# Scores from fp16 pairs in place of fp32r pairs, and an earlier opening of the projection's buffers

## The chip, the cores and the metric

The kernel runs on one core of a Trainium2 chip. The metric is the device time of one execution in microseconds (us); lower is better. The kernel before was timed three times: 886.39, 886.42 and 890.78 us, median 886.42 us. TensorE is PE in the profile, its weight loads are PEld, VectorE is DVE, ScalarE is ACT, GpSimd is POOL, and SyncE (which only issues transfers here) is SP.

## The reference

One layer of an encoder with 2064 tokens (16 meta tokens and 2048 real ones), width 1024, in float32:

```
u = rmsnorm(h, norm_g) @ w_in                # 1024 -> 1984 columns, split in six
pool_in, pool_gate, c_q, c_kv, k_r, attn_gate = split(u)
pool_out = silu(pool_gate) * pool_mixer(pool_in)      # trailing means 2/4/8/16 minus the token
q = rmsnorm(c_q) @ w_q_b                     # 4 heads x (128 plain + 64 rotary)
k, v = split(rmsnorm(c_kv) @ w_kv_b)         # 4 heads x (128 + 128); one shared rotary key from k_r
s = (q_nope.k_nope + q_rope.k_rope) * 192**-0.5
p = softmax(where(key chunk <= query chunk, s, min))  # chunks of 64 tokens, meta tokens ahead
attn_out = silu(attn_gate) * (p @ v)
h = h + concat(pool_out, attn_out) @ w_out
return rmsnorm(h, final_norm_g)[16:]
```

## The kernel before, in words

Precision is kept by splitting a float32 value into a high and a low part and summing three products (high by high, high by low, low by high). Where the parts are `F32R` (a float32 read by TensorE in one pass) they take 4 bytes an element; where they are `F16` they take 2.

The work runs in three stages.

1. **Tokens** (`phase0`, `post0`): in 17 tiles of 128 tokens the latent columns (query 256, key/value 128, rotary 64) are projected from `xh`, `xl` and `wth`, `wtl`. `post0` takes the two norms from a Square on ScalarE and a power on GpSimd, applies the rotation to the shared key, and transposes the result on TensorE. The keys end as a pair in `klo` (keys 0 to 1039) and `khi` (the rest), each with a latent part and a rotary part. `prep_attention` loads the attention weights, and `absorb` multiplies the query and key weights into one matrix per head (`weh`, `wel`), so that a query meets the 128 latent key columns directly. `qprep(g)` makes the queries of 256 tokens as pairs `qh`, `ql` (latent) and `qr` (rotary, high and low in the two halves of the partitions).
2. **Attention rows** (`step(c, p)`: chunk `c` of 64 queries, `p` is a pair of heads, so 128 query rows). `scores` cuts the visible keys into pages of up to 4 tiles and blocks of up to 512 keys. For a block five matmuls add into one PSUM bank (lines 440 to 444), VectorE takes the maximum (446), ScalarE the exponential (467) and its fp16 high part (470), GpSimd or VectorE the low part (472), and SyncE issues a transfer that transposes the page (479). `pv` of the chunk before follows one chunk later and multiplies the transposed pages by the values (503). Six PSUM banks (tag `s`) hold score blocks and projection results in turn. Pages sit in rings of buffers `p`, `hl` and `pt`, drawn from the pools `att1`, `att2` and `att3`; `set_pages` says which pools are in the ring. Chunks 0 to 7 run beside the token stage; then come 23 to 20, 27 to 24, 31 to 28, 19 to 16 (the long rows, in the order of `ORDER`), and 15 down to 8. After chunk 28 `att2` leaves the ring; after chunk 19 (`CLOSE`) it is closed, and the pool `c1` of the projection opens in its place.
3. **Projection** (`pair`, `op_prep`, `op`): the remaining columns of `w_in` in fp16 pairs and the output projection. Its first pieces are put among the rows by two tables: `PREP` says after which chunk weights are loaded (`a`), scaled and split (`b`) and token columns loaded (`x`); `FILL` says after which chunk one `pair` of column groups (48 matmuls of 256) is computed. The order of the rest is the string `TAIL`.

The framework's planner puts the instructions of each engine in a fixed order; each engine then runs its own list in that order, and SyncE's transfers too are issued in order.

Of the kernel before, what the change touches and what calls it, by code (L numbers as in the profile page):

```python
# [8 lines left out]
F32 = mybir.dt.float32  # L9
# [32 lines left out]
ATT2 = (3, 2, 3)  # L42
# [3 lines left out]
FILL = {15: 1, 13: 1, 11: 1}  # L46
# [17 lines left out]
LASTLONG = 28  # L64
CLOSE = 19
# [4 lines left out]
PREP = {18: 'a4', 17: 'b4 x0', 16: 'a5', 15: 'b5', 14: 'x1', 12: 'x2', 10: 'a0'}  # L70
# [21 lines left out]
def hymba(tc, hT, hcat, tab, w_tok, w_m, w_out, wqT, wqr, wkT, wv, pool_w,  # L92
# [38 lines left out]
    nc.gpsimd.memset(inv2[:, 1:2], 1.0 / 128.0)  # L131
# [19 lines left out]
    klo = kv.tile([P, 2, 2, KLO + META], F32R, name="klo")  # L151
    kx_cm, kx = open_pool("kx", side="right")
    khi = kx.tile([P, 2, 2, L - KLO], F32R, name="khi", tag="khi", bufs=1, padded_shape=[P, 2, 2, 1088])
# [11 lines left out]
    gks = kv.tile([P, 1], F32, name="gks")  # L165

# [51 lines left out]
    load_rest(1)  # L218

# [31 lines left out]
    def post0(j):  # L251
# [11 lines left out]
        nc.gpsimd.tensor_scalar(out=st[:T], in0=st[:T], scalar1=EPS, scalar2=None, op0=ALU.add)  # L263
# [12 lines left out]
        nc.scalar.mul(out=vh[:T, j], in_=u[:T, 256:384], mul=SV)  # L276
        nc.vector.scalar_tensor_tensor(out=vl[:T, j], in0=u[:T, 256:384], scalar=SV, in1=vh[:T, j], op0=ALU.mult, op1=ALU.subtract)
# [17 lines left out]
    def prep_attention():  # L295
# [12 lines left out]
    def absorb(wk_r, gk_bc, wq_r, wr_r, wv_r):  # L308
        nc.vector.tensor_scalar(out=gqa, in0=gq_t, scalar1=ALPHA, scalar2=None, op0=ALU.mult)
        nc.vector.tensor_scalar(out=gks, in0=gkv_t, scalar1=UNSCALE, scalar2=None, op0=ALU.mult)  # L310
        nc.vector.tensor_tensor(out=wk_r, in0=wk_r, in1=gk_bc.rearrange("p (o c) -> p o c", o=1).broadcast_to([P, H, P]), op=ALU.mult)
        for i in range(2):
# [5 lines left out]
            nc.vector.scalar_tensor_tensor(out=wel[:, i], in0=pw, scalar=gqa[:, i:i + 1], in1=f(weh[:, i]), op0=ALU.mult, op1=ALU.subtract)  # L318
            nc.scalar.mul(out=wrh[:, i], in_=wr_r[:, i], mul=gqa[:, i:i + 1])
            nc.vector.scalar_tensor_tensor(out=wrl[:, i], in0=wr_r[:, i], scalar=gqa[:, i:i + 1], in1=f(wrh[:, i]), op0=ALU.mult, op1=ALU.subtract)  # L320
# [5 lines left out]
    def qprep(g):  # L326
# [5 lines left out]
        qh = qp.tile([P, 4, H, CH], F32R, name=f"qh{g}", tag="qh", bufs=2)  # L332
        ql = qp.tile([P, 4, H, CH], F32R, name=f"ql{g}", tag="ql", bufs=2)
        qr = qp.tile([P, 4, H, CH], F32R, name=f"qr{g}", tag="qr", bufs=2)
        for hp in range(2):
# [10 lines left out]
            nc.vector.tensor_sub(out=ql[:, :, 2 * hp:2 * hp + 2].rearrange("p c h t -> p h c t"), in0=ps, in1=f(dst))  # L346
# [22 lines left out]
        for s in range(2):  # L369
            for e in range(2):  # L370
# [3 lines left out]
                nc.vector.tensor_sub(out=dst[64:128], in0=src, in1=f(dst[0:64]))  # L374
# [33 lines left out]
    def scores(c, p):  # L408
# [43 lines left out]
        nc.vector.tensor_scalar(out=nb_, in0=nm, scalar1=LNP, scalar2=None, op0=ALU.add)  # L452
        for pg, (base, m, blocks) in enumerate(pages):
# [12 lines left out]
            for o, w, _, _, bi in blocks:  # L466
                nc.scalar.activation(out=pr[:, o:o + w], in_=pss[bi][:, :w], func=AF.Exp, bias=nb_,  # L467
# [89 lines left out]
    def load_x(i):  # L557
        o, n = SUBS[i]
        if i == 0:
            x = cw["pool"].tile([P, 2 * KT * n], F16, name="x0", tag="x0", bufs=1)  # L560
        else:
            if i == 1:
                cw["x"] = kx.tile([P, 2, 4352], F16, name="xx", tag="khi", bufs=1)
            x = cw["x"][:, i % 2, :2 * KT * n]
# [262 lines left out]
    att2_cm, att2 = open_pool("att2", side="right")  # L827
# [22 lines left out]
    flush()  # L850
    close_pool(att3_cm)
# [85 lines left out]
```

## Time and profile before

| | profiled execution |
|---|---|
| its time | 889.79 us |
| its span, first to last instruction | 888.0 us |
| mean granted TensorE clock | 0.978 |
| PE busy | 848.8 us (96%) |
| PEld busy | 684.0 us |
| DVE busy | 536.8 us |
| ACT busy | 480.6 us |
| POOL busy | 321.3 us |

The busy time of PE counts each matmul from its start to its modelled end, and matmuls overlap, so a row's mean is longer than the distance from one matmul's start to the next; rates are read from the distances. A wait row says which engine stood idle at which line, until which instruction, for how long in all, how often, and the longest. The granted clock is 1.00 at 2.4 GHz and 0.50 at 1.2 GHz.

### The profile page before, as it was taken

How to read it: one execution, taken by the hardware profiler on the slowest of the kernel's cores; microseconds unless marked ns; L12 is line 12 of the kernel's file. 1: busy time of each engine (PE TensorE's matmuls, PEld its weight loads, DVE VectorE, ACT ScalarE, POOL GpSimd, SP SyncE). 2: the span in 40 equal slices, each digit the busy share in tenths (PEclk: the TensorE clock that was granted, in tenths of full speed). 3: DMA queues.
4: the chain of work that ended last, by engine and by line, in shares of the span. 5: the costliest groups of instructions: out<-in, count | busy, mean ns of one | idle time of the engine just before them, and what ended most of it. 6: DMA issues, size and time to landing. Idle time of an engine off the chain costs nothing. (4 is left out here: it accounts for less than half of the span.)

```text
span 888.0 us, 16286 instructions
## 1 busy us (share of the span) xinstructions
PE 848.8 (96%) x5835; PEld 684.0 (77%) x5835; DVE 536.8 (60%) x1268; ACT 480.6 (54%) x1268; POOL 321.3 (36%) x512
## 2 busy tenths in 40 slices
PE   9979989999999999898888998999999999999996
PEld 8969968889888888787877897866666666667644
DVE  6657769856757667878624578775455344435242
ACT  6656756757777667785634684854242332232321
POOL 2666642434545453645313124641141121111100
PEclk9989999999999999998999999999999999999998
DMA  8755525977798788884786112212133122111111
GB/s 287 219 170 161 163 46 100 175 145 136 131 148 150 137 153 155 168 156 130 147 180 247 48 55 76 75 26 76 48 90 107 48 72 72 48 49 48 48 40 56
DMA packets 206956, 101.80 MB, mean 115 GB/s; under 512 B 169257, under 2 KB 196363, under 8 KB 206875
## 3 DMA queue, kind: packets, MB, share of 16 engines
q1 hardware_dynamic: 187392, 93.30, 44.0%
q10 hardware_dynamic: 19483, 7.47, 3.7%
q8 instruction: 46, 0.75, 0.4%
q14 instruction: 35, 0.29, 0.1%
HBM read 55.60 MB, written 8.43 MB: 72 GB/s over the span
## 5 line engine op out<-in xcount | busy, mean ns | idle before, releaser
L633 PEld LDWEIGHTS <-w 128*128 128x128 f16 x2304 | 226.8, 99 | 36.7 <-ACT w L617 2.3
L633 PE MATMUL mp<-xx,w 128*128 128x256 f16 x2016 | 229.4, 275 | 0.6 <-DVE gt L662 0.6
L765 PE MATMUL op<-wo,mh 128*128 128x512 f16 (+1 forms) x792 | 168.1, 373 | 0.0
L765 PEld LDWEIGHTS <-mh 128*128 128x128 f16 x792 | 77.5, 98 | 85.5
L472 POOL TENSOR_TENSOR hl<-p,hl 128x512 f16<-128x512 f32 (+4 forms) x104 | 105.0, 1031 | 94.9 <-ACT hl L470 94.8
L467 ACT ACTIVATE p<-s,st 128x512 f32<-128x512 f32 (+8 forms) x168 | 99.4, 600 | 63.2 <-DVE st L452 53.0
L446 DVE TENSOR_REDUCE st<-s 128x1 f32<-128x512 f32 (+6 forms) x154 | 88.7, 589 | 19.0 <-PE s L444 17.5
L503 PE MATMUL o<-pt,vh 128*128 128x256 f16 x544 | 92.2, 274 | 2.3 <-DMA pt<-hl 2.3
L470 ACT CAST hl<-p 128x512 f16<-128x512 f32 (+6 forms) x168 | 82.5, 541 | 4.1 <-DMA pt<-hl 3.9
L769 ACT ACTIVATE osq<-xr 128x512 f16<-128x512 f32 (+1 forms) x33 | 20.4, 617 | 100.0 <-DVE xr L767 78.0
L503 PE MATMUL o<-pt,vl 128*128 128x256 f16 x272 | 74.4, 274 | 0.0
L660 ACT ACTIVATE th<-mp,whalf 128x256 f32<-128x256 f32 x64 | 30.0, 469 | 72.6 <-PE mp L633 58.7
L767 DVE SCALAR_TENSOR_TENSOR xr<-op,mmx,xr 128x512 f32<-128x512 f32 (+1 forms) x33 | 24.2, 734 | 72.4 <-PE op L765 72.4
L503 PEld LDWEIGHTS <-vh 128*128 128x128 f16 x544 | 52.1, 98 | 11.6 <-issue 2.6
L771 POOL TENSOR_SCALAR oss<-oss 128x1 f32<-128x1 f32 x16 | 3.9, 246 | 154.6 <-DVE oss L770 154.6
L472 DVE TENSOR_TENSOR hl<-p,hl 128x512 f16<-128x512 f32 (+7 forms) x64 | 50.6, 792 | 8.1 <-ACT hl L470 7.5
L440 PE MATMUL s<-klo,qh 128*128 128x512 f32 (+9 forms) x116 | 46.2, 398 | 8.5 <-ACT p L467 5.4
L573 DVE SCALAR_TENSOR_TENSOR yr<-yr,gxs,rbc 128x256 f32<-128x256 f32 (+1 forms) x64 | 35.5, 617 | 15.8 <-DMA yr<-hT_in 15.7
L441 PE MATMUL s<-klo,qh 128*128 128x512 f32 (+9 forms) x116 | 43.5, 375 | 0.0
L442 PE MATMUL s<-klo,ql 128*128 128x512 f32 (+9 forms) x116 | 43.5, 375 | 0.0
L444 PE MATMUL s<-klo,qr 128*128 128x512 f32 (+9 forms) x116 | 43.2, 373 | 0.0
L577 POOL TENSOR_TENSOR xx<-yr,xx 128x512 f16<-128x512 f32 x28 | 36.0, 1299 | 19.8 <-ACT xx L576 19.8
(229 smaller groups left out, 1756.6 us busy)
## 6 DMA issues: line engine op xcount, KB each, us to landing
xt<-hcat_in SPq DMA_DIRECT2D x16, 512.0 KB, 6.7
xr<-hcat_in SPq DMA_DIRECT2D x16, 512.0 KB, 3.8
raw<-hT_in SPq DMA_DIRECT2D x15, 512.0 KB, 5.0
out_dram<-xr SPq DMA_DIRECT2D x15, 512.0 KB, 2.7
yr<-hT_in SPq DMA_DIRECT2D x14, 512.0 KB, 3.8
wr<-w_m_in SPq DMA_DIRECT2D x12, 512.0 KB, 4.2
rb<-rd ACTq DMA_DIRECT2D x32, 128.0 KB, 4.6
wor<-w_out_in SPq DMA_DIRECT2D x8, 512.0 KB, 6.5
```

The lines of the kernel that those rows point to most:

```text
L440: nc.tensor.matmul(ps[:, :w], lhsT=q(qh), rhs=kt[:, 0, 0, sl], start=True, stop=False)
L441: nc.tensor.matmul(ps[:, :w], lhsT=q(qh), rhs=kt[:, 1, 0, sl], start=False, stop=False)
L442: nc.tensor.matmul(ps[:, :w], lhsT=q(ql), rhs=kt[:, 0, 0, sl], start=False, stop=False)
L444: nc.tensor.matmul(ps[:, :w], lhsT=q(qr), rhs=kt[:, 1, 1, sl], start=False, stop=True)
L446: nc.vector.reduce_max(out=mx[:, bi:bi + 1], in_=ps[:, :w], axis=AX.X)
L467: nc.scalar.activation(out=pr[:, o:o + w], in_=pss[bi][:, :w], func=AF.Exp, bias=nb_, accum_out=sm[:, bi:bi + 1] if nb > 1 else tot)
L470: nc.scalar.copy(out=hl[:, 0, sl], in_=pr[:, sl])
L472: eng.tensor_tensor(out=hl[:, 1, sl], in0=pr[:, sl], in1=hl[:, 0, sl], op=ALU.subtract)
L503: nc.tensor.matmul(ps[:, :2 * P], lhsT=v, rhs=x, start=i == 0, stop=i == len(ops) - 1)
L577: nc.gpsimd.tensor_tensor(out=xl[:, k:k + 2], in0=xr[:, k - k0:k - k0 + 2], in1=xh[:, k:k + 2], op=ALU.subtract)
L633: nc.tensor.matmul(ps[:, :n - sk], lhsT=a[:, k], rhs=x[:, k, sk:n], start=e == 0, stop=e == 3 * KT - 1)
L765: nc.tensor.matmul(ps[:, :w], lhsT=x[:, k], rhs=y[:, sl], start=i == 0, stop=i == 3 * KT - 1)
```

## The change

Keys (`klo`, `khi`) and queries (`qh`, `ql`, `qr`) become fp16 pairs. The value scale moves into the norm of the key/value latent (`inv2`, `eps2`), the rotary key is scaled by a power of two `kd` taken from the norm of its weight columns, and `absorb` scales the combined query weights by a power of two `tt` taken from the sums of their squares. The exponential then multiplies its input by the inverse, `tinv`, a column of 128 values, and the maximum is scaled likewise. The buffers of the queries are half as large, and the staging of the first tokens and of two weights uses other buffers. `att2` stays open to the end of the rows with two `pt` buffers in place of three, `c1` opens before the long rows, and `PREP` and `FILL` name earlier chunks. The second and third blocks of token columns (`x1`, `x2`) get separate buffers, where one buffer in `khi`'s place held both.

```diff
-ATT2 = (3, 2, 3)
+ATT2 = (3, 2, 2)
-FILL = {15: 1, 13: 1, 11: 1}
+FILL = {19: 1, 15: 1, 11: 1}
-LASTLONG = 28
-CLOSE = 19
-PREP = {18: 'a4', 17: 'b4 x0', 16: 'a5', 15: 'b5', 14: 'x1', 12: 'x2', 10: 'a0'}
+PREP = {20: 'a4', 27: 'b4', 24: 'x0', 31: 'a5', 28: 'b5', 17: 'x1', 13: 'x2', 10: 'a0'}
...
-    klo = kv.tile([P, 2, 2, KLO + META], F32R, name="klo")
+    klo = kv.tile([P, 2, 2, KLO + META], F16, name="klo")
-    khi = kx.tile([P, 2, 2, L - KLO], F32R, ...)
+    khi = kx.tile([P, 2, 2, L - KLO], F16, ...)
...
+    fj = ap.tile([P, KT, 64], F16, name="fj", tag="fj", bufs=1)
+    nc.scalar.activation(out=fj, in_=f(wth[:, :, 384:448]), func=AF.Square, accum_out=fk[:, 0:1])
+    pf = bank("m", "pf")
+    nc.tensor.matmul(pf[:, 0:1], lhsT=ones, rhs=fk[:, 0:1], start=True, stop=True)
+    ...  (maximum on DVE, power on POOL, three more on DVE: kd and its inverse)
...
-        nc.gpsimd.tensor_scalar(out=st[:T], in0=st[:T], scalar1=EPS, scalar2=None, op0=ALU.add)
+        nc.gpsimd.tensor_tensor(out=st[:T], in0=st[:T], in1=eps2[:T], op=ALU.add)
+        nc.gpsimd.tensor_scalar(out=rk, in0=r, scalar1=kd[:T], scalar2=None, op0=ALU.mult)
...
-        wr_r = ap.tile([P, 2, 256], F32, name="wr_r", tag="raw", bufs=2, padded_shape=[P, 2, 512])
+        wr_r = qp.tile([P, 2, 256], F32, name="wr_r", tag="qr", bufs=2)
-        wv_r = ap.tile([P, H, P], F32, name="wv_r", tag="raw", bufs=2, padded_shape=[P, KT, P])
+        wv_r = qp.tile([P, H, P], F32, name="wv_r", tag="ql", bufs=2)
...
     # absorb, per half i, after the four matmuls into pw:
-            nc.scalar.mul(out=weh[:, i], in_=pw, mul=gqa[:, i:i + 1])
+            for e, src in ((4, pw), (6, wr_r[:, i])):
+                nc.scalar.activation(out=junk, in_=src, func=AF.Square, scale=gqa[:, i:i + 1], accum_out=fk[:, e + i:e + i + 1])
     # absorb, once:
+        nc.tensor.matmul(pf[:, 0:4], lhsT=ones, rhs=fk[:, 4:8], start=True, stop=True)
+        ...  (two on DVE, power on POOL, six on DVE: tt, tinv, gqe, gqr)
+        for i, pw in enumerate(pws):
+            nc.scalar.mul(out=weh[:, i], in_=pw, mul=gqe[:, i:i + 1])
...
-        qh = qp.tile([P, 4, H, CH], F32R, name=f"qh{g}", tag="qh", bufs=2)
+        qh = qp.tile([P, 4, H, CH], F16, name=f"qh{g}", tag="qh", bufs=2)      # ql, qr likewise
...
-        nc.vector.tensor_scalar(out=nb_, in0=nm, scalar1=LNP, scalar2=None, op0=ALU.add)
+        nc.vector.tensor_scalar(out=nb_, in0=nm, scalar1=tinv, scalar2=LNP, op0=ALU.mult, op1=ALU.add)
-                nc.scalar.activation(out=pr[:, o:o + w], in_=pss[bi][:, :w], func=AF.Exp, bias=nb_,
+                nc.scalar.activation(out=pr[:, o:o + w], in_=pss[bi][:, :w], func=AF.Exp, scale=tinv, bias=nb_,
...
-    att2_cm, att2 = open_pool("att2", side="right")
+    att2_cm, att2 = open_pool("att2", side="left")
+    c1_cm, c1 = open_pool("c1", side="right")
+    pre_c(c1)
...
-        if c == LASTLONG:
-            set_pages((att1, ATT1), (att3, ATT3))
-        if c == CLOSE:
-            close_pool(att2_cm)
-            c1_cm, c1 = open_pool("c1", side="right")
-            pre_c(c1)
```

## Rows read from the trace of the kernel before

**Rows 1.** Busy time, clock and DMA share in three stretches (us).

```profile
core 0: us, PE busy (x) PEld busy (x) DVE busy (x) ACT busy (x) POOL busy (x), PEclk, DMA share, GB/s
38.00:56.00 18.00, 12.39 (x66) 10.84 (x66) 11.13 (x29) 13.20 (x37) 10.72 (x23) 0.85 0.59 174
150.00:344.00 194.00, 191.26 (x1272) 168.69 (x1271) 134.79 (x318) 138.27 (x396) 90.39 (x115) 1.00 0.83 150
344.00:464.00 120.00, 107.07 (x789) 94.97 (x788) 82.88 (x202) 75.49 (x213) 53.21 (x68) 0.94 0.73 146
```

**Rows 2.** Timeline of PE, score matmuls in long rows: start, length (us), instruction.

```profile
294.81 0.34 PE L440 MATMUL s<-khi,qh 128*128 128x384 f32 x1
...
295.69 0.38 PE L440 MATMUL s<-khi,qh 128*128 128x464 f32 x1
...
296.76 0.39 PE L440 MATMUL s<-klo,qh 128*128 128x512 f32 x1
...
297.91 0.39 PE L440 MATMUL s<-klo,qh 128*128 128x512 f32 x1
...
308.58 0.28 PE L440 MATMUL s<-khi,qh 128*128 128x272 f32 x1
...
309.20 0.39 PE L440 MATMUL s<-klo,qh 128*128 128x512 f32 x1
```

**Rows 3.** Timeline of PE, fp16 matmuls of the projection, unbroken runs merged.

```profile
585.76 1.91 PE L633 MATMUL mp<-xx,w 128*128 128x256 f16 x16
587.51 4.70 PE L765 MATMUL op<-wo,mh 128*128 128x512 f16 x21
```

**Rows 4.** Line 440 (first of five matmuls of a block): ns min/median/max, widths.

```profile
L440 PE MATMUL s<-klo,qh x116: 281/393/689, 61.7 to 444.1; 128*128 128x512 f32 x68, 128*128 128x384 f32 x12, 128*128 128x272 f32 x8, 128*128 128x336 f32 x6
...
L440 PE MATMUL s<-khi,qh x52: 199/338/497, 145.7 to 353.9; 128*128 128x384 f32 x12, 128*128 128x272 f32 x8, 128*128 128x464 f32 x6, 128*128 128x400 f32 x6
```

**Rows 5.** ACT by line and form: busy us, mean ns, idle before.

```profile
L467 ACT ACTIVATE p<-s,st 128x512 f32<-128x512 f32 x72 | 48.9, 685 | 51.3 <-DVE st L452 44.0 <-DMA rb<-rd 4.2 <-POOL hl L472 1.7
...
L467 ACT ACTIVATION_READ_ACCUMULATOR p<-s,st 128x1 f32 x168 | 33.9, 202 | 0.0
...
L664 ACT ACTIVATE gt<-mp,winv 128x256 f32<-128x256 f32 x32 | 14.9, 466 | 0.0
...
L505 ACT CAST oh<-o 128x256 fp32r<-128x256 f32 x32 | 12.0, 375 | 11.1 <-PE o L503 10.9
```

**Rows 6.** ACT by line, 344 to 464 us.

```profile
L467 ACT ACTIVATE p<-s,st 128x384 f32<-128x384 f32 (+7 forms) x40 | 23.0, 578 | 10.7 <-DVE st L452 6.4 <-DVE hl L472 2.6 <-issue 1.5
...
L590 ACT ACTIVATE wa<-wr 128x512 f16<-128x512 f32 x6 | 3.8, 642 | 4.8 <-DMA wr<-w_m_in 4.8
L617 ACT ACTIVATE w<-wr,wsc 128x512 f16<-128x512 f32 x4 | 2.9, 714 | 2.8 <-DVE wsc L89 2.8
...
L576 ACT CAST x<-yr 128x544 f16<-128x544 f32 x4 | 2.6, 646 | 0.0
```

**Rows 7.** The load of `x0` on DVE, 325 to 470 us.

```profile
L573 DVE SCALAR_TENSOR_TENSOR yr<-yr,gxs,rbc 128x272 f32<-128x272 f32 x8 | 4.9, 668 | 1.6 <-DMA yr<-hT_in 1.5
```

**Rows 8.** Waits of PE, 400 to 450 us: total, times, longest (us).

```profile
PE s L440 <- ACT p L467: 3.4, 2, 2.6
PE s L440 <- ACT gt L664: 3.1, 1, 3.1
```

**Rows 9.** Waits, 38 to 56 us.

```profile
PE pt L280 <- DVE u L274: 5.3, 2, 5.1
```

**Rows 10.** Small operations by line, whole span: busy us, mean ns, idle before.

```profile
L264 POOL TENSOR_TENSOR st<-st,expo 128x2 f32<-128x2 f32 (+1 forms) x17 | 13.2, 778 | 1.1
...
L452 DVE TENSOR_SCALAR st<-st 128x1 f32<-128x1 f32 x64 | 9.3, 147 | 0.8
```

**Rows 11.** Waits of SP's queue, whole span.

```profile
SPq L571 <- DVE w L618: 21.0, 2, 11.4
...
SPq L178 <- DMA wr_r<-wqr_in: 5.1, 1, 5.1
```

More of the change, by code (lines that the diff above doesn't have):

```diff
@@ L165, in hymba @@
     gks = kv.tile([P, 1], F32, name="gks")
+    ones = kv.tile([P, P], F32, name="ones")
+    nc.gpsimd.memset(ones, 1.0)
+    fk = kv.tile([P, 16], F32, name="fk")
+    gqe = kv.tile([P, 2], F32, name="gqe")
+    gqr = kv.tile([P, 2], F32, name="gqr")
+    kd, tt, tinv = fk[:, 2:3], fk[:, 12:13], fk[:, 13:14]
     q_cm, qp = open_pool("qp", side="left")
@@ L316, in absorb @@
                     nc.tensor.matmul(pw[:, h], lhsT=wq_r[:, h, i * P:(i + 1) * P], rhs=wk_r[:, h], start=True, stop=True)
-            nc.scalar.mul(out=weh[:, i], in_=pw, mul=gqa[:, i:i + 1])
-            nc.vector.scalar_tensor_tensor(out=wel[:, i], in0=pw, scalar=gqa[:, i:i + 1], in1=f(weh[:, i]), op0=ALU.mult, op1=ALU.subtract)
-            nc.scalar.mul(out=wrh[:, i], in_=wr_r[:, i], mul=gqa[:, i:i + 1])
-            nc.vector.scalar_tensor_tensor(out=wrl[:, i], in0=wr_r[:, i], scalar=gqa[:, i:i + 1], in1=f(wrh[:, i]), op0=ALU.mult, op1=ALU.subtract)
+            for e, src in ((4, pw), (6, wr_r[:, i])):
+                junk = ap.tile([P, 512], F16, name=f"fj{i}_{e}", tag="fj", bufs=1)
+                junk = junk.rearrange("p (h c) -> p h c", h=H) if e == 4 else junk[:, 0:256]
+                nc.scalar.activation(out=junk, in_=src, func=AF.Square, scale=gqa[:, i:i + 1], accum_out=fk[:, e + i:e + i + 1])
@@ new lines, in absorb @@
+            pws.append(pw)
+        pf = bank("s", "pf2")
+        nc.tensor.matmul(pf[:, 0:4], lhsT=ones, rhs=fk[:, 4:8], start=True, stop=True)
+        nc.vector.reduce_sum(out=fk[:, 8:10], in_=pf[:, 0:4].rearrange("p (a b) -> p a b", b=2), axis=AX.X)
+        nc.vector.tensor_scalar(out=fk[:, 8:10], in0=fk[:, 8:10], scalar1=1e-30, scalar2=None, op0=ALU.max)
+        nc.gpsimd.tensor_tensor(out=fk[:, 8:10], in0=fk[:, 8:10], in1=expo, op=ALU.pow)
+        nc.vector.tensor_scalar(out=fk[:, 8:10].bitcast(I32), in0=fk[:, 8:10].bitcast(I32), scalar1=0x7F800000, scalar2=None, op0=ALU.bitwise_and)
@@ new lines, in absorb @@
+        nc.vector.tensor_scalar(out=gqr, in0=gqa, scalar1=tt, scalar2=fk[:, 3:4], op0=ALU.mult, op1=ALU.mult)
+        for i, pw in enumerate(pws):
+            nc.scalar.mul(out=weh[:, i], in_=pw, mul=gqe[:, i:i + 1])
+            nc.vector.scalar_tensor_tensor(out=wel[:, i], in0=pw, scalar=gqe[:, i:i + 1], in1=f(weh[:, i]), op0=ALU.mult, op1=ALU.subtract)
+        for i in range(2):
+            nc.scalar.mul(out=wrh[:, i], in_=wr_r[:, i], mul=gqr[:, i:i + 1])
+            nc.vector.scalar_tensor_tensor(out=wrl[:, i], in0=wr_r[:, i], scalar=gqr[:, i:i + 1], in1=f(wrh[:, i]), op0=ALU.mult, op1=ALU.subtract)
@@ L561, in load_x @@
         else:
-            if i == 1:
-                cw["x"] = kx.tile([P, 2, 4352], F16, name="xx", tag="khi", bufs=1)
-            x = cw["x"][:, i % 2, :2 * KT * n]
+            if i < 3:
+                cw["x", i] = kx.tile([P, 2 * KT * G], F16, name=f"xx{i}", tag="xa" if i == 1 else "khi", bufs=1,
+                                     padded_shape=[P, 2 * KT * G if i == 1 else 4352])
+            x = cw["x", 2 - i % 2]
         x = x.rearrange("p (a k t) -> p a k t", a=2, k=KT)
@@ L850, in hymba @@
     flush()
+    close_pool(att2_cm)
     close_pool(att3_cm)
```

44 lines of the change are left out of this document (29 added, 15 removed).

## The prediction, made before the kernel after was run

> **What bounds the kernel now.** I read the stretches first, then the timeline of TensorE, then the waits. In the long rows, 150 to 344 us, PE is busy 191.26 of 194 us at a clock of 1.00, while ACT has 138.27, DVE 134.79 and the transfer engines a share of 0.83 [rows 1]: the stage lasts as long as its matmuls do. In 344 to 464 us, the end of the long rows and the short ones, PE is idle for 12.9 of 120 us and the clock is 0.94 [rows 1]; 0.94 means 12% of the time, some 14 us, at the lower level, where a busy PE loses half, so up to 7 us more. Some 20 us are lost there. The reader sees why in the waits: score matmuls stand until ACT has emptied a bank, once behind an exponential and once behind a gate of a `pair` [rows 8]; ACT and DVE carry the pieces of the projection (`a`, `b`, `x`, `pair`) beside the rows. The third place is 38 to 56 us: PE is busy 12.39 of 18 us, and 5.1 us of that idle time is one wait for a tile on DVE [rows 1, 9]. From about 550 us on the projection runs back to back, and the change doesn't touch its matmuls.
>
> **A. The score matmuls.** Five matmuls of a block start 0.88 us (384 keys), 1.07 us (464), 1.15 us (512) and 0.62 us (272) ahead of the next block [rows 2]: 176, 214, 230 and 124 ns each. Fp16 ones of 512 take (4.70 − 0.39) / 20 = 215.5 ns and of 256 (1.91 − 0.28) / 15 = 109 ns [rows 3], the last one's length taken from a like one [rows 2]. Between them a straight line gives 116 (272), 162 (384) and 195.5 (464). So fp16 saves 15 ns at 512, 14 at 384, 18 at 464 and 8 at 272. There are 116 + 52 = 168 blocks, 840 matmuls: 72 blocks of 512 (4 of them in `khi`), 24 of 384, 72 of other widths [rows 4]. 72 × 5 × 15 ns = 5.4 us; 24 × 5 × 14 = 1.7; 72 × 5 × 12 (between 8 and 18) = 4.3. Sum 11.4; bounds 840 × 8 = 6.7 and 840 × 18 = 15.1. Nearly all long blocks lie where PE alone sets the pace, so the gain counts: −11 us.
>
> The distance of the fp32r matmuls is 230 ns per 512 columns, that of the fp16 ones 215.5 [rows 2, 3]. The Trainium skill, "TensorE: Matmul & The Clock Gate", section "Back-to-back issue gap", gives one law for the distance, columns through the full clock plus about 2.5 ns, and no term for the type. By it a score block would take the same time in either type and term A would be nothing, which is a rival below. The trace agrees with the law for fp16 (215.5 ns) and disagrees for fp32r (230 ns).
>
> **B. The stretch from 344 to 464 us.** What leaves it for the long rows: on ACT four absolute sums of `a5` (4 × (642 + 202 ns) = 3.4 us), the splits `b4` and `b5` (three groups of four, 2.9 us for the one shown, 8 in all) and `x0` (2.6), together 14 of 75.5 us; on DVE `x0` (4.9) and the low parts of the splits (taken like one group of ACT's, 3), 8 of 82.9 [rows 1, 5 to 7]. `x1`, `x2`, `a0` and the last two pairs stay; the first pair moves to chunk 19. The ring keeps `att2`, so 7, 9 and 9 buffers serve the short rows where 4, 7 and 7 did; transposed pages wait less. What is late next is the chain from maximum to exponential, and that becomes longer: the exponential reads its scale from a column. The trace has no activation with two columns; with one column an activation of 256 takes 466 ns and a cast without takes 375 [rows 5]. I take the same 91 ns for the second column, from nothing to 91 ns. 40 exponentials lie here [rows 6], so 3.6 us go back to ACT. Of 20 us lost I take 6 back; the bounds are 14 (all but the start of the projection) and −5 (DVE, at 83 of 120 us, still blocks in `x1` and `x2`, and all of the 3.6 us shows).
>
> ScalarE's gates with one column take 91 ns more than casts without one [rows 5]. The Trainium skill, "ScalarE: Activation LUTs", section "What ACT_TABLE_LOAD costs", states that each such column adds about 93 ns to an activation; the trace agrees for the first column, and no row shows a second. It speaks against this change: by it the 168 exponentials cost ScalarE an estimated 15.6 us more.
>
> **C. The start.** `absorb` gains four Squares with sums (two of 512, two of 256: 2 × 0.71 + 2 × 0.47 + 4 × 0.2 = 3.2 us on ACT [rows 5, 6]), a matmul, eight small ones on DVE (8 × 0.147 = 1.2) and a power on POOL (0.78) [rows 10]; with the handovers about 6 us stand between the weights' product and `weh`, on which the first `qprep` waits. Behind the waiting Squares on ACT stand the casts of the next token tile; behind the power on POOL, the norms. In 38 to 56 us PE has 5.6 us idle [rows 1] that can hide the 6 us if the planner puts token tiles ahead, so the cost is 0 to 6, and another 2 if the clock stays low. Each token tile gets one more POOL operation for `rk` (17 × about 0.2 us); POOL is busy 10.72 of 18 there. Against it, `wr_r` and `wv_r` leave the buffers of the token tiles: SP's wait of 5.1 us for `wr_r` before a token load goes [rows 11], worth 0 to 4 us. I take +3, bounds −4 and +8. The sum for the rotary key after the first four tiles (one Square, one matmul, a power, four on DVE) lies beside loads; it is inside these bounds.
>
> **D. The long rows with more in them.** They receive the 14 us on ACT and 8 us on DVE of B, plus 91 ns for most of the other 128 exponentials, up to 12 us. ACT comes to about 138 + 14 + 11 = 163 us of 194 − 9 = 185, 88%; DVE to 143, 77%. PE stays the bound on the mean, but a split comes in bursts of about 4 us on ACT, and the six banks hold five to six blocks, so a burst can stand PE for one or two us. Five bursts: 0 to 8 us, I take +1.5, since the waits in the trace of that kind are few in the long rows (PE idle 2.7 us in all [rows 1]). The three megabytes of weights and tokens meet a DMA share of 0.83, at a quicker pace 0.87; the nine `pt` buffers (ten before) just hold the five pages of chunk 31 and the four of chunk 24.
>
> **Sum.** −11.4 − 6 + 3 + 1.5 = −12.9 us. On the profiled execution: span 888.0 becomes 875.1, its time of 889.8 becomes 876.9. That execution stands 3.4 us above the median of the runs shown, so the median goes from 886.4 to 873.5 us. With all bounds at once it would be 852 to 895; the terms are independent, and I take 859 to 883 for this case.
>
> **Rivals.**
> 1. *The rate doesn't change.* Something other than the type paces five matmuls into one bank. For it: one law for all types. Against: the two distances in the same trace. It leaves −6 + 3 + 1.5 = −1.5: 885 us. 6%.
> 2. *ACT becomes the bound.* The second column and the moved pieces bring ACT to 88% on the mean, and in chunks near a `b` over 100%; then the 11 us are paid back at the banks. For it: the waits on ACT [rows 8]. Against: ACT's own waits, 6.4 us on the maximum in 344 to 464 us [rows 6]. About 882 us, half of it on either side of the bound below. 10%.
> 3. *Slower: SP's queue.* Weight and token loads now stand among the transposes of the long rows. A load that waits for its staging buffer holds every transpose behind it; such waits took 21.0 us for two where they occur now [rows 11], about 10.5 each. The lag of one chunk covers the scores of a chunk, two pairs of 384 + 464 + 2 × 512, 8.5 us [rows 2]. It decides once the wait is over what is left of this lag: with half of it in use already, four waiting loads cost 4 × (10.5 − 4.3) = 25 us more, 899 us. For it: the queue is in order, and two staging buffers serve six loads. Against: the new places lie two or more rows apart. 8%.
> The forecast has the remaining 76%.
>
> **How the numbers follow.** About 0.5%, 4.4 us, can be told from no change, so faster means below 882.0 us. The forecast's case lies below it but for a tail of 3%; rival 2 adds 5%: faster 0.78. Same: the tail, rival 1 and half of rival 2, 0.14. Slower: rival 3, 0.08. The range goes from 858 to 885 us: rival 3 and the lowest and highest tails are left out.
>
> **What would show it.** A: lines 440 to 444 at 215 to 217 ns per 512 keys; wrong, if above 225. B: PE idle in the stretch before the projection under 10 us and its clock above 0.96; exponentials of 512 at about 775 ns in place of 685 [rows 5] show the second column. C: no new wait of PE on `weh`, `wel` over 3 us. D: PE idle in the long rows under 5 us; wrong, if line 440 waits on line 467 or 617 there, or line 503 on transposes behind a load. The prediction as a whole is wrong if the score distances fall and the span doesn't.

## The result and the profile after

The changed kernel takes 917.13 us in the median (910.29 to 919.23, four runs), the kernel before beside it 887.88 us (886.39 to 890.78): ratio 1.031, 95% interval 1.025 to 1.038. The forecast was 873.5 us, range 858 to 885: a gain was forecast, and the kernel became slower.

The profiled execution took 918.24 us, its span is 916.5 us, the clock over it 0.962 (0.978 before). Stretches of the kernel after, columns as in [rows 1]:

```profile
core 0: us, PE busy (x) PEld busy (x) DVE busy (x) ACT busy (x) POOL busy (x), PEclk, DMA share, GB/s
0.00:75.00 75.00, 63.89 (x321) 56.99 (x322) 40.67 (x112) 43.47 (x105) 39.51 (x95) 0.91 0.63 200
75.00:165.00 90.00, 81.94 (x503) 67.57 (x501) 65.14 (x208) 58.80 (x182) 45.46 (x99) 0.94 0.50 125
165.00:225.00 60.00, 56.73 (x384) 38.51 (x383) 39.52 (x96) 44.25 (x119) 25.96 (x35) 1.00 0.79 144
225.00:275.00 50.00, 36.56 (x238) 26.32 (x237) 37.34 (x80) 35.34 (x89) 27.50 (x31) 0.90 0.81 157
275.00:355.00 80.00, 78.24 (x556) 55.62 (x554) 53.01 (x122) 63.61 (x164) 38.58 (x47) 1.00 0.79 133
355.00:425.00 70.00, 56.47 (x373) 40.66 (x372) 45.21 (x108) 38.68 (x105) 31.28 (x41) 0.85 0.66 135
425.00:475.00 50.00, 50.00 (x391) 38.62 (x389) 36.65 (x106) 37.28 (x109) 15.87 (x29) 1.00 0.78 126
```

In the long rows before, PE idled 2.7 of 194 us at a clock of 1.00 [rows 1]. Now two stretches stand out: 225 to 275 us (PE idle for 13.4 of 50 us, clock 0.90) and 355 to 425 us (13.5 of 70, clock 0.85). The start, 0 to 75 us, is at 63.89 busy; before it was 67.88:

```profile
0.00:75.00 75.00, 67.88 (x363) 61.23 (x364) 47.04 (x117) 47.10 (x112) 40.66 (x92) 0.95 0.72 224
```

PE's busy time over the whole span (first row of the page) is all but that of before, 848.8 us:

```profile
PE 847.4 (92%) x5839; PEld 630.1 (69%) x5839; DVE 536.3 (59%) x1280; ACT 497.7 (54%) x1278; POOL 327.9 (36%) x534
```

Yet the score matmuls need some 14 us less (below), so an estimated 12 us are what matmuls took longer at the lower of the clock's two levels. PE's idle time, the span less its busy time, grew from 39.2 to 69.1 us. The 28.5 us of the span are thus about −14 of matmuls, +12 of clock and +30 of idle time.

What the score matmuls do is as forecast. Timeline of PE after, as in [rows 2]:

```profile
300.28 0.36 PE L478 MATMUL s<-khi,qh 128*128 128x464 f16 x1
...
301.26 0.38 PE L478 MATMUL s<-klo,qh 128*128 128x512 f16 x1
...
302.34 0.38 PE L478 MATMUL s<-klo,qh 128*128 128x512 f16 x1
```

Five matmuls of 512 keys take 1.08 us, 216 ns each, in place of 230; of 464 keys 0.98, 196 ns in place of 214. The exponentials, by form, as in [rows 5]:

```profile
L505 ACT ACTIVATE p<-s,st,fk 128x512 f32<-128x512 f32 x72 | 55.5, 776 | 36.0 <-DVE st L490 25.9 <-issue 5.5 <-DMA pt<-hl 3.7
```

776 ns against 685: the second column costs 91 ns, the value taken from the gates.

Waits of PE over the whole span (total, times, longest, us); before, the longest wait of this kind near the row end was 2.6 us [rows 8]:

```profile
PE s L478 <- ACT p L505: 19.9, 8, 7.5
PE qt L406 <- POOL qra L402: 8.6, 4, 5.7
PE av L565 <- DVE ol L544: 3.9, 1, 3.9
PE o L541 <- DMA pt<-hl: 3.5, 1, 3.5
PE qp L392 <- DVE ql L384: 3.4, 1, 3.4
PE we L336 <- DVE klo L308: 3.1, 1, 3.1
```

PE stood 10.1 us for exponentials in 225 to 275 us. The timeline of DVE there shows what the exponentials stood behind (start, length, us; in brackets idle time and its releaser):

```profile
249.60 1.28 DVE L484 TENSOR_REDUCE st<-s 128x1 f32<-128x512 f32 x2
250.80 0.81 DVE L514 TENSOR_TENSOR hl<-p,hl 128x16 f16<-128x16 f32 x1
254.39 2.30 DVE L612 SCALAR_TENSOR_TENSOR yr<-yr,gxs,rbc 128x272 f32<-128x272 f32 x4 [2.78 <-DMA yr<-hT_in]
256.61 0.14 DVE L519 TENSOR_REDUCE rs<-st 128x1 f32<-128x4 f32 x1
256.68 5.03 DVE L612 SCALAR_TENSOR_TENSOR yr<-yr,gxs,rbc 128x272 f32<-128x272 f32 x4
261.63 0.68 DVE L510 TENSOR_TENSOR hl<-p,hl 128x512 f16<-128x512 f32 x1
...
263.63 0.82 DVE L484 TENSOR_REDUCE st<-s 128x1 f32<-128x256 f32 x2
264.49 0.16 DVE L489 TENSOR_REDUCE st<-st 128x1 f32<-128x4 f32 x1
264.68 0.21 DVE L490 TENSOR_SCALAR st<-st,fk 128x1 f32<-128x1 f32 x1
```

This is `x0`, put behind chunk 24. Its eight products stand in DVE's queue ahead of the row's next maxima, and the first of them waits 2.78 us for the token load. From 250.8 to 263.6 us no maximum is taken; the bias (L490) comes at 264.68 us, no exponential can start, no bank comes free, PE stands. Nothing here is a lack of DVE time on the mean (37.34 of 50 us busy): it is an order in which the urgent work is last. PE pays for it twice:

```profile
257.98 0.38 PE L482 MATMUL s<-klo,qr 128*128 128x512 f16 x1
265.85 0.37 PE L478 MATMUL s<-khi,qh 128*128 128x256 f16 x1 [7.49 <-ACT p L505]
266.01 0.42 PE L479 MATMUL s<-khi,qh 128*128 128x256 f16 x1
266.23 0.42 PE L480 MATMUL s<-khi,ql 128*128 128x256 f16 x1
```

Behind the wait of 7.49 us, matmuls of 256 keys start 0.22 us apart; ahead of it, at 255 us, five of them took 0.55 us, 0.11 each. So PE ran at the clock's lower level there (0.90 over the stretch).

At 361 to 387 us it is `x1`. Its products wait on DVE for their loads, ahead of the rotation of the next queries and of the rows' work, and PE stands 5.7 us for `qra`, 3.9 for `ol` and 1.1 for `at`, 10.7 of the 13.5 us idle there:

```profile
362.07 1.67 DVE L612 SCALAR_TENSOR_TENSOR yr<-yr,gxs,rbc 128x256 f32<-128x256 f32 x4 [3.84 <-DMA yr<-hT_in]
...
377.01 3.42 DVE L612 SCALAR_TENSOR_TENSOR yr<-yr,gxs,rbc 128x256 f32<-128x256 f32 x4 [2.40 <-DMA yr<-hT_in]
```

### The profile page after: what moved, and what is told of

Its sections match the earlier page's. It is cut to its first block, busy times and chain, and to the rows that moved or that the text cites. A ratio compares the mean times of both kernels' runs of the same rounds, so it can differ in the third digit from the quotient of the medians.

```text
span 916.5 us, 16320 instructions
## 1 busy us (share of the span) xinstructions
PE 847.4 (92%) x5839; PEld 630.1 (69%) x5839; DVE 536.3 (59%) x1280; ACT 497.7 (54%) x1278; POOL 327.9 (36%) x534
## 5 line engine op out<-in xcount | busy, mean ns | idle before, releaser
L505 ACT ACTIVATE p<-s,st,fk 128x512 f32<-128x512 f32 (+8 forms) x168 | 114.5, 691 | 48.3 <-DVE st L490 36.1
L541 PE MATMUL o<-pt,vh 128*128 128x256 f16 x544 | 97.7, 283 | 3.8 <-DMA pt<-hl 3.5
L484 DVE TENSOR_REDUCE st<-s 128x1 f32<-128x512 f32 (+6 forms) x154 | 88.5, 589 | 16.2 <-PE s L482 15.1
L541 PE MATMUL o<-pt,vl 128*128 128x256 f16 x272 | 76.8, 282 | 0.0
L541 PEld LDWEIGHTS <-vh 128*128 128x128 f16 x544 | 54.9, 102 | 14.6 <-DMA pt<-hl 4.0
L510 DVE TENSOR_TENSOR hl<-p,hl 128x512 f16<-128x512 f32 (+7 forms) x64 | 42.7, 669 | 15.6 <-ACT hl L508 15.2
L612 DVE SCALAR_TENSOR_TENSOR yr<-yr,gxs,rbc 128x256 f32<-128x256 f32 (+1 forms) x64 | 37.8, 650 | 23.8 <-DMA yr<-hT_in 22.2
L478 PE MATMUL s<-klo,qh 128*128 128x512 f16 (+9 forms) x116 | 41.4, 357 | 5.4 <-ACT p L505 5.4
L766 POOL TENSOR_TENSOR at<-at,gt 128x256 f32<-128x256 f32 x32 | 23.7, 740 | 53.0 <-DVE gt L704 37.0
L480 PE MATMUL s<-klo,ql 128*128 128x512 f16 (+9 forms) x116 | 41.3, 356 | 0.0
L479 PE MATMUL s<-klo,qh 128*128 128x512 f16 (+9 forms) x116 | 41.3, 356 | 0.0
```

The costliest lines, as they stand in the source:

```text
L478: nc.tensor.matmul(ps[:, :w], lhsT=q(qh), rhs=kt[:, 0, 0, sl], start=True, stop=False)
L479: nc.tensor.matmul(ps[:, :w], lhsT=q(qh), rhs=kt[:, 1, 0, sl], start=False, stop=False)
L480: nc.tensor.matmul(ps[:, :w], lhsT=q(ql), rhs=kt[:, 0, 0, sl], start=False, stop=False)
L484: nc.vector.reduce_max(out=mx[:, bi:bi + 1], in_=ps[:, :w], axis=AX.X)
L510: eng.tensor_tensor(out=hl[:, 1, sl], in0=pr[:, sl], in1=hl[:, 0, sl], op=ALU.subtract)
L541: nc.tensor.matmul(ps[:, :2 * P], lhsT=v, rhs=x, start=i == 0, stop=i == len(ops) - 1)
```

## The experiments

Each was timed beside runs of the kernel before on the same chip; ratios are to those, with the 95% interval in brackets. "Old" means as in the kernel before.

### Which part costs the 29 us

**late_pieces**: the changed kernel with `PREP`, `FILL`, `ATT2`, `LASTLONG`, `CLOSE` and the opening of `c1` old.

```diff
-PREP = {20: 'a4', 27: 'b4', 24: 'x0', 31: 'a5', 28: 'b5', 17: 'x1', 13: 'x2', 10: 'a0'}
+PREP = {18: 'a4', 17: 'b4 x0', 16: 'a5', 15: 'b5', 14: 'x1', 12: 'x2', 10: 'a0'}
...
+LASTLONG = 28
+CLOSE = 19
...
```

> The kernel after, with the opening of the projection's buffers and the chunks of all pieces as in the kernel before (att2 leaves the ring after chunk 28 and closes after 19, old PREP and FILL, three pt buffers). Theory L (the pieces among the long rows, the token columns x0 and x1 above all, hold VectorE and ScalarE ahead of the rows' maxima and exponentials, and PE stands): the stalls of 7.5 us at chunk 24 and of 15 us around chunk 17 go, 917 falls by 20 to 28 us, to 889-897. Theory E (the second column of the exponential, 91 ns on each of 168, makes ScalarE late everywhere): the stalls stay with the rows, 908-917. Theory S (start: absorb's longer chain and the moved loads cost 12 us by score matmul 100): that matmul stays at about 158 us in the trace either way, and the rest of the loss with it.

899.51 us, ratio 1.013 [1.010, 1.016], between the expectations. Over half of the loss goes with the moved work and the early opening, and still 12 us are left: the scores in fp16 and the start are not a gain by themselves.

**const_scales**: the changed kernel with `kd` = 4 and `tt` = 128 written as constants; the sums of squares, their matmuls and the powers are left out.

```diff
-    ...  (fj, pf, junk: squares, matmuls by ones, powers)
+    for ap_, v in ((kd, 4.0), (fk[:, 3:4], 0.25), (tt, 128.0), (tinv, 1.0 / 128.0)):
+        nc.gpsimd.memset(ap_, v)
```

> The kernel after, with the powers of two written as constants in place of being computed: no Squares, no two small matmuls, no power in absorb or behind the first tiles; the rest of the computation is kept. Theory S1 (the chain in absorb delays weh and with it the token stage): score matmul 100 moves from 158 to about 150 us, time 907-911. Theory S2 (the loads of wr_r and wv_r, moved to the very start, and the staging do it): matmul 100 stays at 155-158, time 914-918.

912.44 us, 1.028 [1.024, 1.031]: some 5 us less than the changed kernel, with intervals that overlap, and between the two expectations.

**open_early_late_pieces**: only `PREP` and `FILL` old; `c1` opens early and `att2` stays.

> The kernel after, only PREP and FILL as in the kernel before: the buffers open before the long rows and att2 stays with two pt buffers, but the pieces come at the old chunks. Theory L (the place of the pieces): within 5 us of the run with everything late, 885-897, the better half if the longer ring helps the short rows. Rival R (the opening itself: nine pt buffers where there were ten, other memory): stays at 912-918.

907.96 us, 1.022 [1.020, 1.024], between the expectations again. That is 8.5 us over late_pieces, and the intervals lie apart.

**weights_early_x_late**: the changed kernel with the pieces of x later, and with `FILL` old, since the first `pair` multiplies `x0`.

```diff
-FILL = {19: 1, 15: 1, 11: 1}
+FILL = {15: 1, 13: 1, 11: 1}
...
-PREP = {20: 'a4', 27: 'b4', 24: 'x0', 31: 'a5', 28: 'b5', 17: 'x1', 13: 'x2', 10: 'a0'}
+PREP = {20: 'a4', 27: 'b4', 31: 'a5', 28: 'b5', 17: 'x0', 14: 'x1', 12: 'x2', 10: 'a0'}
```

> The changed kernel with its early opening and its early weight pieces (a4 at 20, b4 at 27, a5 at 31, b5 at 28), but the pieces of x in the short rows as before (x0 at 17, x1 at 14, x2 at 12). The changed kernel took 917 us, the one with all pieces late 908. If the pieces of x cost it (DVE's eight products of L612 ahead of a row's maxima, POOL's share ahead of the queries' additions): 907 to 911 us. If the weight pieces cost it (ACT's and POOL's splitting inside the longest rows): 913 to 918 us.

902.73 us, 1.017 [1.013, 1.022], lower than either theory said, and 14 us less than the changed kernel (the intervals lie apart). The stretch that had stood out:

```profile
225.00:275.00 50.00, 46.55 (x328) 33.24 (x327) 32.10 (x82) 40.73 (x108) 25.57 (x33) 0.97 0.80 153
```

PE is busy 46.55 of 50 us, where it was 36.56, though ACT has more to do (40.73 us in place of 35.34). So it was what `x0` does on DVE there, not ACT's load.

**late_old_staging**: late_pieces with `wr_r`, `wv_r` and the first tiles in their old buffers.

> late_pieces with the buffers of wr_r, wv_r and the first tiles as in the kernel before; the chain in absorb is kept. Theory S2 (moved loads and staging): 899.5 falls to 892-895, near fp16_alone, and score matmul 100 to 147-149 us. Theory S1 (the chain): 897-901 and matmul 100 at 151-152 us.

896.47 us, 1.010 [1.008, 1.013]: 3 us less than late_pieces, with intervals that overlap, and between the two expectations; the new staging is not the gain that term C booked.

**const_x_late**: weights_early_x_late with the constants of const_scales.

> weights_early_x_late (902.7 us) with the powers of two as constants, so without the chain in absorb. If the parts add up: 4 to 5 us less, 897.5 to 899 us, and the two early openings of the weights' splitting hide nothing of the chain. If the chain is hidden once the rows are disturbed elsewhere: 901 to 904 us.

904.24 us, 1.019 [1.015, 1.024]: no gain. The small parts don't add up, and 0 to 5 us is all that can be said of the chain in `absorb`.

Several expectations ask when score matmul 100 starts. The profiled execution of each kernel gives it, from the timeline of PE (starts of the 100th and the last of the 840, end of the span, us):

```
                          100th   840th    span   span less 100th
before                    145.2   444.8   888.0        742.8
fp16_alone (below)        146.1   444.3   890.3        744.2
late_old_staging          149.8   449.0   894.6        744.8
late_pieces               150.9   450.8   899.3        748.4
weights_early_x_late      150.9   453.7   900.9        750.0
const_x_late              152.5   454.1   900.4        747.9
const_scales              153.7   464.3   907.6        753.9
open_early_late_pieces    157.8   460.2   906.9        749.1
changed kernel            157.9   470.2   916.5        758.6
```

Two readings that the medians suggest don't hold against it. The early opening is not shown to cost 8.5 us: 7 of them are there at the 100th score matmul, and weights_early_x_late, which opens as early, has 150.9 us there. Nor are the early x pieces shown to cost 14 us. With constants in both kernels the same step is 8.2 us (912.44 against 904.24), and of the 14 us, 7 are there at the 100th score matmul, some 100 us ahead of the first x piece. Up to that matmul the changed kernel, open_early_late_pieces and weights_early_x_late run the same instructions in the same order on every engine. What differs is waits and clock: over the first 75 us it is 0.91 in the changed kernel and 0.98 in weights_early_x_late (row below), and at 146 to 150 us of open_early_late_pieces PE waits 3.0 us for exponentials and then runs at the lower level, 256 keys 0.21 us apart. Why one kernel meets this and another doesn't stays open.

```profile
0.00:75.00 75.00, 66.50 (x347) 59.10 (x348) 44.12 (x121) 47.49 (x115) 43.29 (x102) 0.98 0.69 216
```

Behind the 100th score matmul the early x pieces, with the first `pair`, cost 8.6 us (758.6 against 750.0), with constants 6.0 (753.9 against 747.9); the early opening and the early weight pieces cost 0.7 and 1.6 us more than late_pieces. Each figure is of one execution.

### Why the faster scores bring nothing

**fp16_alone**: constants, old staging, old pieces; what is left of the change is fp16 and the column in the exponential.

> Both undone at once and the staging as in the kernel before: fp16 pairs and the exponential with a column as scale, constants for the powers of two, buffers of wr_r, wv_r and the first tiles as before, all pieces late. If the rate gain of the score matmuls (13 us by the two traces) counts nearly in full: 873-880. If the second column of the exponential eats it (theory E): 882-890.

892.34 us, 1.005 [1.002, 1.007]: slower than before, above both expectations.

**fp16_imm**: the same with the scale as an immediate.

```diff
-    func=AF.Exp, scale=tinv, bias=nb_
+    func=AF.Exp, scale=1.0 / 128.0, bias=nb_
```

> fp16_alone with the exponential's scale as a constant in the instruction in place of a column: no second column, exponentials back at about 685 ns for 512. Theory E (the 91 ns on 168 exponentials, 15 us of ScalarE, paid back the gain of the score matmuls): 892 falls to 877-884. Theory O (what is given back are stalls from a changed order on engines that work strictly in order, not ScalarE's load): 888-894.

891.25 us, 1.004 [1.002, 1.006], as theory O had it. The column is not what eats the gain.

**before_scale_column**: the kernel before with a column of ones as the exponential's scale.

> The kernel before with only a column of ones as the exponential's scale. Theory E: the column alone costs 6 us or more, 894-902. Theory O (ScalarE has slack in the long rows): 887-892.

893.20 us, 1.006 [1.004, 1.008], between the two. By form, an exponential of 512 (line 469 here):

```profile
L469 ACT ACTIVATE p<-s,st,tinv 128x512 f32<-128x512 f32 x72 | 55.6, 777 | 47.5 <-DVE st L454 40.2 <-DVE st L448 3.8 <-DVE wsc L89 3.4
```

ACT has 15 us more, and some 5 of it show.

**types_only**: the kernel before with `klo`, `khi`, `qh`, `ql`, `qr` in fp16, in buffers of the old sizes and places; the scaling is left out.

```diff
-    klo = kv.tile([P, 2, 2, KLO + META], F32R, name="klo")
+    klo = kv.tile([P, 2, 2, KLO + META], F16, name="klo")
```

> The kernel before with only the types of klo, khi, qh, ql and qr changed to fp16; buffers padded to the old sizes, no scaling at all (the scaling that keeps them in fp16's range is left out). If the 13 us of the score matmuls count: 874-880. Theory O: the stalls between rows take part of it back, 881-889.

888.0 us, 0.999 [0.996, 1.001]. This is term A by itself. The score matmuls are faster by somewhat more than forecast: the 840 of them, each at the usual distance from start to start of its width in the trace, add up to 158.9 us before and 145.1 here. The time is the same; PE's idle time is 50.5 us in the profiled execution, where it was 39.2. Waits of PE here:

```profile
PE s L440 <- ACT p L467: 9.5, 8, 3.3
PE pt L280 <- DVE u L274: 6.1, 3, 3.3
PE qt L368 <- POOL qra L364: 5.8, 4, 2.6
PE qa L342 <- DVE ol L506: 3.7, 1, 3.7
```

Before, the first was 6.3 us and the third 1.7.

```profile
PE s L440 <- ACT p L467: 6.3, 6, 2.6
...
PE qa L342 <- DVE ol L506: 2.6, 1, 2.6
...
PE qt L368 <- POOL qra L364: 1.7, 1, 1.7
```

From here two theories: TensorE sets the pace and an accident of order hid the gain, or the rows have a second bound close behind, the maxima on DVE that every exponential waits for. The next four tell them apart.

**four_score_matmuls**: the fifth score matmul is left out, which is more than twice as much PE time as the types gave.

```diff
-                nc.tensor.matmul(ps[:, :w], lhsT=q(qr), rhs=kt[:, 0, 1, sl], start=False, stop=False)
-                nc.tensor.matmul(ps[:, :w], lhsT=q(qr), rhs=kt[:, 1, 1, sl], start=False, stop=True)
+                nc.tensor.matmul(ps[:, :w], lhsT=q(qr), rhs=kt[:, 0, 1, sl], start=False, stop=True)
```

> The kernel before with the fifth score matmul (L444) left out of all 168 blocks; everything else as before. 168 matmuls at 184 ns from start to start are 31 us of TensorE. Theory P (TensorE alone sets the pace of the rows; that types_only gained nothing is an accident of its order): 855 to 863 us. Theory W (in the rows TensorE is only a little later than the other engines' fixed chain of maxima, exponentials, casts and transposes, so a shorter score stage turns into waits): most of the 31 us comes back, 868 to 884 us, with longer waits 's <- ACT p' and 'qt <- POOL qra'.

881.14 us, 0.993 [0.990, 0.996], in theory W's range. Of 31 us, 6 show.

**types_short_max**: types_only with each block's maximum over 64 columns; the exponential's factor and bias are set so that values stay finite. The bias is still read from the maxima, times nought, so each exponential waits for them as before.

```diff
-                    nc.vector.reduce_max(out=mx[:, bi:bi + 1], in_=ps[:, :w], axis=AX.X)
+                    nc.vector.reduce_max(out=mx[:, bi:bi + 1], in_=ps[:, :64], axis=AX.X)
```

> types_only with each block's maximum taken over its first 64 columns only (and a bias of nought, a factor of 0.001 in the exponential, so that the values stay finite); the same instructions otherwise. DVE's L446 falls from 589 ns to about 130 in 154 cases, 70 us of DVE, and every exponential can begin about 0.45 us sooner. Theory W in its form 'maximum, then exponential, is the chain': the 13 us of the faster score matmuls now show, 868 to 878 us. Rival Q (the waits come from the preparation of queries and the low parts, not from the maxima): 882 to 890 us.

874.91 us, 0.985 [0.981, 0.990], in the range of theory W. Line 446 on DVE:

```profile
L446 DVE TENSOR_REDUCE st<-s x154: 207/218/226, 135.8 to 422.6; 128x1 f32<-128x64 f32 x154
```

**before_short_max**: the same maxima in the kernel before.

> The kernel before (fp32r score matmuls) with only the maxima over 64 columns of types_short_max (bias of nought, factor 0.001). Theory W2 (maxima and matmuls each hide the other: neither alone shows): 882 to 888 us, so that the two together are worth more than the sum of each. Rival M (the maxima alone set the pace, the matmuls nothing): 872 to 878 us, as types_short_max. In between, 878 to 882, both share.

881.06 us, 0.992 [0.989, 0.995]. Below W2's 882 to 888, in the range where both share.

**four_matmuls_short_max**: both cuts.

> The kernel before with the fifth score matmul left out and the maxima over 64 columns. four_score_matmuls took 881.1 us for 31.6 us less matmul time. If the maxima are what gave that back: 855 to 865 us. If something else in the rows did (transposes, exponentials, the preparation of queries): 868 to 876 us.

858.34 us, 0.968 [0.962, 0.973], as expected if the maxima gave the time back. With the other five, as medians, and PE's idle time in the profiled executions (span less busy time):

```
                           maxima whole   over 64 columns   difference
five matmuls, fp32r        887.2 - 888.0       881.1          -7
five matmuls, fp16         888.0               874.9         -13
four matmuls, fp32r        881.1               858.3         -23

PE idle, us
five matmuls, fp32r         39.2                37.2
five matmuls, fp16          50.5                40.5
four matmuls, fp32r         55.5                40.9
```

Down a column: with whole maxima 31 us of matmuls bring 6; with short ones 23. Along a row: the less PE has to do, the more the maxima bring. Each hides the other: that is what two bounds close together look like. The idle times say it without the clock: shorter score stages raise PE's idle time by 11 and 16 us with whole maxima, by 3 and 4 with short ones. The rest of what short maxima bring is clock. In before_short_max PE idles about as long as before, and what falls is its busy time, from 848.8 to 841.1 us for the same matmuls, at a granted clock of 0.989 in place of 0.978. Stretch 140 to 400 us, columns as in [rows 1]: the kernel before, types_only, four_score_matmuls, then the last with short maxima.

```profile
140.00:400.00 260.00, 253.15 (x1730) 224.24 (x1730) 189.06 (x460) 187.20 (x533) 119.98 (x155) 0.99 0.81 148
```

```profile
140.00:400.00 260.00, 246.13 (x1726) 176.54 (x1725) 181.26 (x460) 188.05 (x535) 117.00 (x155) 0.98 0.82 148
```

```profile
140.00:400.00 260.00, 238.95 (x1618) 207.28 (x1618) 180.19 (x459) 187.53 (x530) 120.25 (x156) 0.97 0.84 152
```

```profile
140.00:400.00 260.00, 247.24 (x1721) 215.08 (x1721) 150.72 (x489) 200.55 (x564) 134.86 (x171) 0.98 0.87 161
```

PE idles 6.9 us, then 13.9, then 21.1, and its clock falls from 0.99 to 0.97: what the matmuls give up comes back in good part as idle time. With DVE relieved the idle time falls to 12.8 and PE gets through 1721 matmuls in the stretch in place of 1618. With four matmuls and whole maxima DVE was busy for only 69% of it, ACT for 72%: neither looks like a bound by its share. A cut of ACT's exponentials or casts as large as that of the maxima (50 to 57 us of DVE) was not run, so whether other links of the chain would bring as much is not shown.

**types_lows_on_pool** and **before_lows_on_pool**: the low part of each row's first block on POOL in place of DVE.

```diff
-LPOOL = (0, 1, 1, 1, 1)
+LPOOL = (1, 1, 1, 1, 1)
```

> types_only with the low part of each row's first block (64 L472 at 792 ns on DVE) moved to POOL, where the other 104 of them are; nothing left out. DVE loses 50 us in the rows, POOL gains some 66 (1029 ns each). If DVE's load as a whole delays the maxima: 876 to 884 us, below both kernels. If only the latency of a block counts, or POOL is late next: 886 to 894 us.

> The kernel before with the same move of the first block's low part to POOL. Control for types_lows_on_pool: 886 to 892 us by either theory, since TensorE is the bound there as much as DVE.

886.79 us, 0.999 [0.996, 1.001], and 889.96 us, 1.003 [1.001, 1.006]. No version faster than both comes from this. In types_lows_on_pool the waits for exponentials fall, those for transposed pages and for the projection's weights rise:

```profile
PE o L503 <- DMA pt<-hl: 6.3, 4, 3.6
PE mp L633 <- ACT w L617: 5.1, 2, 2.9
...
PE s L440 <- ACT p L467: 2.9, 3, 1.6
```

Whether POOL is late next or only the delay of a block's own maximum counts stays open.

**types_add_on_dve**: the addition that ends the queries' rotary part moves from POOL to DVE.

> types_only with the addition that ends the rotary part of the queries (L364, POOL) moved to DVE. The wait 'qt <- POOL qra' was 5.8 us in types_only and 1.7 before. Theory Q: that wait goes and takes 3 to 5 us with it, 881 to 884 us. Theory W (another engine of the same chain is late next): 885 to 890 us.

886.70 us, 0.998 [0.996, 1.001]: the wait `qt <- POOL qra` can be removed and nothing follows; another took its place, as theory W said.

**before_one_memset**: the kernel before with a memset that nothing reads.

> The kernel before with one more tile of 128x1 and one memset of it on POOL at the start, which nothing reads. Control for the small differences: if the static order follows the work and not such details, 885 to 890 us, ratio within 0.3% of one. If a detail that shifts the planned order is worth as much as the 3 to 5 us told of the column, the staging and the chain, it lies outside that.

889.38 us, 1.002 [1.000, 1.004], within the 0.3% of the expectation. Differences of 0.4 to 0.6% between versions are near that; one control does not say how much other shifts can make. Part of the spread within one kernel is clock: of the 15 executions of the kernel before beside before_short_max, the fastest took 884.13 us at a granted clock of 0.988, the slowest 892.82 at 0.977.

## Why the prediction was wrong

**A, −11.4 us: the rate was right, the premise failed.** The matmuls got faster by 13.8 us at the trace's own distances, inside the bounds of 6.7 and 15.1; rival 1 is out. (The 2.4 us over the forecast are the blocks of 80 to 208 keys, booked at 8 to 18 ns a matmul, which save 22 to 76.) The step that failed is "the stage lasts as long as its matmuls do". It was read from PE's share, 191.26 of 194 us [rows 1]. That share says that PE was seldom idle, not what would come next: types_only shows nothing of the gain, four_score_matmuls 6 of 31 us, and the two kernels with fewer or faster matmuls and short maxima show where it went. ACT's row of before had the sign of it: 51.3 us idle ahead of the exponentials of 512, 44.0 of them for DVE's L452, the end of the chain of maxima [rows 5]. Rival 2 named ACT's load instead, and priced the waits at the banks as a mishap of bursts; it came near the mechanism but at the wrong engine: cutting ACT's second column (15 us of ACT) in fp16_imm brought 1 us, cutting DVE's maxima (50 us of DVE) 13.

The law that rival 1 leans on is, in the section of the Trainium skill that the prediction names ("TensorE: Matmul & The Clock Gate", section "Back-to-back issue gap"), the gap of an isolated matmul, with about 131 ns given for 512 columns in a sustained stream. The streams here run at 216 ns (fp16) and 230 ns (fp32r); no run shows 131.

**B, −6 us: not seen as a sum.** The last 50 us before the projection did become what it said (425 to 475 us: PE 50.00 busy, clock 1.00, no wait on gates), but in 355 to 425 us PE idled for 13.5 us, most of it at `x1`. The early weight pieces are not shown to win anything: against open_early_late_pieces they are 5 us lower (902.7 against 908.0, intervals that overlap a little), but behind the 100th score matmul the two are alike (750.0 and 749.1 us). The second column was priced exactly. The Trainium skill, "ScalarE: Activation LUTs", section "What ACT_TABLE_LOAD costs", states about 93 ns for such a column; the trace agrees for the second one too, with 91 ns.

**C, +3 us, bounds −4 and +8: right sign, too small in the kernel as it ran.** The 100th score matmul of the changed kernel starts 12.7 us later than before. Chain and staging account for 5 to 6 of them (150.9 in late_pieces against 145.2; by the medians 0 to 5 and 3), inside the bounds. The other 7 came with no instruction that C could have counted, and weights_early_x_late doesn't have them: they are waits and a lower clock (0.91 over the first 75 us, 0.98 there), and what set them off stays open. Term C booked the staging as a gain because SP's wait of 5.1 us would go. PE has waits on `we` there, 3.1 us at the longest, just over the 3 us that it set as the mark.

**D, +1.5 us, bounds 0 to 8: mis-sized.** The x pieces and the first `pair`, moved early, cost 6 to 9 us behind the 100th score matmul and 8 to 14 by the medians, near or above the upper bound. D counted bursts of about 4 us on ACT against six banks. The burst that mattered was on DVE, 10 us long with its wait for a load (251.6 to 261.7 us), and ahead of the maxima in the queue. Its mark, "wrong, if line 440 waits on line 467", is what the trace shows (line 478 on 505, 7.5 us).

**The clock was no term of the sum for the changed kernel.** The prediction priced it in the kernel before, for 344 to 464 us and the start; with the waits of the changed kernel it fell from 0.978 to 0.962, an estimated 12 us (see the result).

**Rival 3, slower by SP's queue:** right outcome, for another reason. At `x0` SP's queue shows no wait at the `yr` loads (at `x1` one of 5.0 us); it was DVE that waited for the load, and what stood behind it there were the maxima.

The parts as measured, in steps from the kernel before: fp16 with its column +4 (892.3), chain +4 (896.5), staging +3 (899.5), opening and weight pieces +3 (902.7), x pieces and first `pair` +14 (917.1), of which 7 lie in the start, where no piece runs. Only the last step is well above the control, and const_x_late shows that the small ones don't add. The forecast missed, then, first of all by A, whose 11 us never came, then by the start and by D. What of the +4 of fp16_alone over types_only is left beyond the column (the extra POOL operation for `rk` in each tile, `eps2`) was not taken apart.

## What to carry to other kernels

A busy share of 98% says that an engine is seldom idle, not that time taken from it shows: before a saving is booked, ask which chain runs beside it in the same stage and how much slack that chain has, for which the idle time ahead of the next engine's instructions and its releaser is the place to look. When work is moved between stages, its load on the mean is the lesser question; ask on each in-order engine what is queued behind it, and whether its first instruction waits for a load. Look at the granted clock beside the idle time: here a wait of 7.5 us was followed by matmuls at half the rate, and the clock took an estimated 12 of the 28.5 us lost. And before a difference of two versions is put down to an edit, see where along the span it arises: half of the 14 us lay ahead of everything that the edit had moved. To find a second bound, cut each suspect alone and both together; the sum of the single cuts (−6 and −7 here, −30 together) tells it.

## What had not been expected of the hardware

A maximum over 64 columns still takes 218 ns on DVE, where about 130 had been expected. One over 512 takes 684 in the kernel before (DVE by form), so an eighth of the columns costs a third of the time; from the two, an estimated 1.04 ns a column and 151 ns that don't depend on the width:

```profile
L446 DVE TENSOR_REDUCE st<-s 128x1 f32<-128x512 f32 x72 | 48.8, 684 | 8.8 <-PE s L444 8.3
```

Narrow matmuls gain most from fp16. Those of 80 keys start 0.11 us apart in the kernel before and 0.03 in types_only (before, then types_only):

```profile
61.74 0.28 PE L440 MATMUL s<-klo,qh 128*128 128x80 f32 x1
61.85 0.28 PE L441 MATMUL s<-klo,qh 128*128 128x80 f32 x1
```

```profile
62.64 0.20 PE L440 MATMUL s<-klo,qh 128*128 128x80 f16 x1
62.67 0.20 PE L441 MATMUL s<-klo,qh 128*128 128x80 f16 x1
```

Over the trace, fp32r matmuls of 80, 144 and 208 keys all start about 112 ns apart; in fp16 it is 36, 63 and 89.
